# An adaLN block with gated convolution and differential attention: shorter lead of the high halves, a later head step, 1024-column pieces, tokens in two transfers, modulation in two bursts

## The chip, the cores and the metric

The kernel runs on one core of a Trainium2 chip. The metric is the device time of one execution in microseconds (us). Three runs of the kernel before gave 950.05, 951.05 and 951.22 us, a median of 951.05. Everything is float32 at the interface. The profile is of one further execution of the same program.

## The reference, cut to what matters

The input is 256 latent tokens `x` and 256 context tokens `ctx`, both of width 2048, with one condition vector each.

```python
shift, scale, gate = split(silu(c) @ w_ada + b_ada, 3)          # w_ada: 2048 x 6144
c_shift, c_scale, _ = split(silu(c_ctx) @ w_ada + b_ada, 3)
h  = rms(x)   * (1 + scale)   + shift
hc = rms(ctx) * (1 + c_scale) + c_shift
p   = h @ w_in                                                  # w_in: 2048 x 12288
pkv = hc @ w_in[:, K and V columns]                             # context gives keys and values only
q, k, v = heads(p);  k, v = concat with context's k, v;  q, k rotated by 2-D axial rope
a = softmax(q1 k1) - lam * softmax(q2 k2);  o = rms(a @ v) * subln_w * (1 - lam_init)
y_b = (o * silu(p[zb])) @ w_out_b                               # 8 heads, 2 x 64 wide
y_a = (gb * conv3(gc * xa) * silu(za)) @ w_out_a                # xa, gb, gc, za: 1024 columns each
m   = sigmoid(p[ga]) * y_a + sigmoid(p[gb]) * y_b
out = rms(x + gate * (m @ w_o)) * final_norm_w
```

## The kernel before, in words

Every large product is computed in three float32r passes. A weight piece is split into a high half (`hi`, a cast on ACT) and a low half (`lo`, piece minus `hi`, a subtraction on DVE). The activations are split in the same way, and TensorE (PE) sums hi times hi, hi times lo and lo times hi. `H` holds the split modulated latents, `hc` (tiles `hctx`) those of the context.

The weights stream from HBM in pieces of 512 KB, which SP issues. Pieces that are split go to tiles `raw` (`RAWB` = 5 buffers), pieces of `w_ada` for the modulation go to tiles `raw_ada` (`ADAB` = 6 buffers). Until the context tokens are transposed, the code allows one raw_ada and two raw buffers less, since context tokens lie in them.

The order of the program is a list `plan`, filled by `do(function)` and `use(piece, function)`, and walked by `run_plan`. Before each piece is used, `advance(done)` emits what is due ahead of it: the cast to `hi` of pieces up to `done + split - held`, the subtraction to `lo` of pieces up to one less, and DMA issues into every free buffer. Each engine executes its instructions in the order in which they are emitted, so this walk sets the order on ACT, DVE and SP as well as on PE. `split` is 1 at the start and `AHEAD` = 4 from the first key piece on; `held` counts the first pieces that are kept until the context needs them.

The stages in order of time are these. First the latent tokens (four transfers of 512 KB) are transposed (`transpose_tokens`), and their mean squares are taken on DVE. Four pieces of `w_ada` give scale and shift of row tile 0. The keys and values of row tile 0 come next (`first_keys`, `first_values`; pieces named `first`), in four pieces of one row tile by 512 columns; then the context tokens are transposed, and the same four pieces serve the context. After that the remaining 15 row tiles of 128 rows are taken in groups (`GROUPS`): row tiles 1, 2 and 3 one at a time, then six pairs. In each group `key_steps` and `value_steps` list the work, in halves j = 0 and 1 of 512 columns, and the modulation pieces of the next group (`ada_items`, tiles `ada`, `arow`, `adat`) are placed between these steps, two pieces at a time. At the end of a group's accumulation DVE adds each PSUM bank to `kT` or `vv`.

Then come the queries (`q`), and the stages zb, xa, gc, gb, za, each made of pieces of two row tiles by 512 columns, 24 matmuls per piece. The 16 units of attention (8 heads by 2 token halves) are woven into these pieces: a new unit starts every `ATTS` = 5 pieces, and its steps `scores`, `exps`, `shares`, `combine`, `probs_t`, `mix` follow at a lag of 0, 1, 2, 3, 4 and 6 pieces. `combine` (DVE) writes `e`, `probs_t` transposes it on PE (`aT`), and `mix` multiplies it with the values (`o`). The merge and the output projection end the kernel.

DMA completion is counted in eight semaphores (`DMAHW0` to `DMAHW7` in the order listings), taken in turn by the transfers of SP and ACT; a transfer waits until the earlier one with its semaphore has landed.

Of the kernel before, what the change touches and what calls it, by code (L numbers as in the profile page):

```python
# [10 lines left out]
F32 = mybir.dt.float32  # L11
F32R = mybir.dt.float32r
# [25 lines left out]
STAT = 2  # L38
NORM, LATE = 88, 96
GATE0, GATES = 97, 2.4  # L40
# [26 lines left out]
def block_kernel(ctx: ExitStack, tc: tile.TileContext, x, c, cx, c_ctx, w_ada, b_ada, w_in, conv_w,  # L67
# [42 lines left out]
    def piece(w, k0, nk, c0, name, dst=None):  # L110
        return (w, k0, nk, c0, 512, name, True, dst)

# [3 lines left out]
    room = {True: RAWB, False: ADAB}  # L116
    lead = {"split": 1, "held": 0}
    rest = []
# [4 lines left out]
    def run_plan():  # L123
# [6 lines left out]
        def advance(done):  # L130
            while True:
                n = state["hi"]
                if n in raws and n < done + lead["split"] - lead["held"] + 1:
                    nk, _, _, name, two, dst = loads[n][2:]
                    if two:
                        parts[n] = dst() if dst else (
                            wp.tile([P, nk, 512], F32R, tag="hi", name=f"hi_{name}", bufs=HIB), None)
                        A.copy(parts[n][0], raws[n])  # L138
                    state["hi"] += 1
                    continue  # L140
                n = state["lo"]
                two, dst = loads[n][6:] if n < state["hi"] else (False, None)
                if n < state["hi"] and n < done + (lead["split"] - lead["held"] if two or dst else AHEAD):
                    if two:
                        hi, lo = parts[n]
                        if not dst:
                            nk, name = loads[n][2], loads[n][5]
                            lo = wp.tile([P, nk, 512], F32R, tag="lo", name=f"lo_{name}")
# [38 lines left out]
    rot = one.tile([P, 2 * T], F32, tag="rot", name="rot")  # L187
    nc.scalar.dma_start(cst, consts[:, 0:C_COS])
    cosT, sinT = rot[:, 0:T], rot[:, T:2 * T]
# [5 lines left out]
    def load_tokens(s, t):  # L195
        for n in range(2):
            if s == 0:
                if n == 0:
                    whole = one.tile([P, 2, half], F32, tag=f"vv{t}", name=f"xin{s}{t}")
                xin = whole[:, n]  # L200
            else:
                pool, tag, bufs = ((wp, "raw", RAWB), (wp, "raw", RAWB), (p1, "ada", ADAB), (p1, "hctx", 2))[t * 2 + n]
                xin = pool.tile([P, half], F32, tag=tag, name=f"xin{s}{t}{n}", bufs=bufs)
            nc.sync.dma_start(xin, (x, cx)[s][0, t * P:(t + 1) * P, n * half:(n + 1) * half])
            xins[s, t, n] = xin

# [7 lines left out]
    cv = one.tile([NC, P], F32, tag="kT0", name="cv")  # L214
    vec = one.tile([NV, P], F32, tag="kT1", name="vec")
    nc.scalar.dma_start(cv[0:16, :], c.rearrange("b (k p) -> (b k) p", p=P))
    nc.scalar.dma_start(cv[16:32, :], c_ctx.rearrange("(k p) -> k p", p=P))
# [199 lines left out]
    def first_keys(parts, j, s):  # L417
        for ct in range(4):
            pb = bank(f"k_{j}{ct}{s}")
            key_mms(pb, parts, 0, ct, s, 0, True, True)  # L420
            A.copy(kT[j]()[:, ct, s, :], pb[:, s * T:(s + 1) * T])

    def first_values(parts, j, s):
        for b in (2 * s, 2 * s + 1):
            pb = bank(f"v_{j}{b}")
            value_mms(pb, parts, 0, b, 0, True, True)
            A.copy(vv[j]()[:, b, :], pb)

    def key_steps(k0, nk, j):

        box, held, last = {}, [], k0 + nk

        def step(kk, per, s, ct):
            parts = held[(kk - k0) // 2]
            if (s, kk) == (0, k0):
                box[ct] = bank(f"k{k0}_{j}{ct}")
            for i in range(per):
                key_mms(box[ct], parts, i, ct, s, kk + i, kk + i == k0, kk + i == last - 1)
            if s and kk + per == last:
                dst = kT[j]()[:, ct].rearrange("p s t -> p (s t)")  # L440
                V.tensor_tensor(dst, box[ct], dst, op=ALU.add)  # L441

        out = []
# [7 lines left out]
    def value_steps(k0, nk, j):  # L451
        box, held = {}, []

        def step(kk, per, b):
            if kk == k0:
                box[b] = bank(f"v{k0}_{j}{b}")
            for i in range(per):
                value_mms(box[b], held[-1], i, b, kk + i, kk + i == k0, kk + i == k0 + nk - 1)
            if kk + per == k0 + nk:
# [4 lines left out]
        for kk, per in cuts(k0, nk):  # L464
            out.append((piece(w_in[0], kk, per, V_OFF + j * 512, f"v{j}_{kk}"), held.append))
            out += [(None, lambda _, a=(kk, per, b): step(*a)) for b in range(4)]
# [69 lines left out]
    held = []  # L536
    for n, (off, j) in enumerate(((K_OFF, 0), (K_OFF, 1), (V_OFF, 0), (V_OFF, 1))):
        def first(parts, f=(first_keys, first_values)[n // 2], j=j):
            f(parts, j, 0)
            held.append((f, parts, j))  # L540
            lead["held"] += 1

        use(piece(w_in[0], 0, 1, off + j * 512, f"first{n}"), first)

# [3 lines left out]
    def first_context(n):  # L548
        f, parts, j = held[n]
        f(parts, j, 1)  # L550
        lead["held"] -= 1

# [13 lines left out]
    for n, g in enumerate(GROUPS[1:]):  # L566
        nxt, tails = [], {}
        if n + 2 < len(GROUPS):
            (scale, scale_end), (shift, shift_end) = ada_items(*GROUPS[n + 2], 1), ada_items(*GROUPS[n + 2], 0)
            nxt = scale + shift  # L570
        kv = key_steps(*g, 0) + key_steps(*g, 1) + value_steps(*g, 0) + value_steps(*g, 1)
        done, total = 0, len(nxt)
        for i, it in enumerate(kv):
# [393 lines left out]
```

## Time and profile before

| | us |
|---|---|
| median of three runs | 951.05 |
| lowest and highest run | 950.05 and 951.22 |
| profiled execution | 951.32 |
| its span, first to last instruction | 949.5 |
| PE busy in it | 922.2 |
| DVE busy in it | 647.9 |
| ACT busy in it | 422.0 |

The profiled execution's time is 1.8 us above its span; this is the launch around it. The page divides the span into 40 slices. Where an engine has idle time, the rows give it in brackets after the instruction that ended it, with the engine or transfer whose event released it. The granted clock of TensorE is given as a share of 2.4 GHz: 1.00 is that level, and 0.50 is 1.2 GHz.

### The profile page before, as it was taken

To read this page: it belongs to the slowest core of one execution; us is meant where nothing else is said; L and a number is where in the kernel's file an instruction comes from. 1 tells how busy PE (TensorE), PEld (TensorE's weight loads), DVE (VectorE), ACT (ScalarE), POOL (GpSimd) and SP (SyncE) were. 2 spreads that over 40 slices of the span, in tenths; PEclk is the share of its full clock that TensorE was granted. 3 is DMA by queue.
4 is the path that set the end of the run, shared out by engine and by line. 5 is a ranking of instruction groups with operands and counts; after the bars stand their busy time and mean duration, and the time that the engine had idled before them with its cause. 6 is when DMAs were issued, how large, how long until landed. Compare 5 with 4: busy or idle time off the path is not lost.

```text
span 949.5 us, 17652 instructions
## 1 busy us (share of the span) xinstructions
PE 922.2 (97%) x7308; PEld 853.1 (90%) x7308; DVE 647.9 (68%) x967; ACT 422.0 (44%) x623; POOL 1.9 (0%) x7
## 2 busy tenths in 40 slices
PE   8699999999999999999999999999999999999996
PEld 7577788888899999999999999999999999998885
DVE  3369866777758676686776866677767667756664
ACT  4442222123234466654765566543543344444442
POOL 0000000000000000000000000000000000000000
PEclk9799999999999999999999999999999999999999
DMA  9687966675366546545454645567987887867552
GB/s 287 207 245 250 342 223 218 214 241 156 89 190 182 179 137 197 156 135 169 149 172 133 180 154 164 167 227 252 312 270 240 304 296 242 288 213 266 178 177 89
DMA packets 123430, 196.76 MB, mean 207 GB/s; under 512 B 6125, under 2 KB 47446, under 8 KB 122838
## 3 DMA queue, kind: packets, MB, share of 16 engines
q1 hardware_dynamic: 122752, 194.40, 64.6%
q8 instruction: 57, 0.93, 0.4%
q10 hardware_dynamic: 598, 1.23, 0.3%
q14 instruction: 23, 0.19, 0.1%
HBM read 193.52 MB, written 2.10 MB: 206 GB/s over the span
## 4 chain that ended last, share of the span: by engine, by line
PE 89%; DVE 5%; DMA 3%; ACT 2%; SPq 1%; issue 1%; ACTq 0%; DVEq 0%
PE gb L484 13%; PE ga L484 10%; PE f L862 9%; PE v L408 9%; PE k L415 9%; PE za L484 5%; PE zb L484 5%; PE yb L484 5%; PE q L484 5%; PE ya L484 5%; PE gc L484 4%; PE xa L484 4%; PE ada L351 3%; DMA raw_first<-in_w_in_dram 1%; PE o L682 1%; SPq L167 1%
## 5 line engine op out<-in xcount | busy, mean ns | idle before, releaser
L484 PE MATMUL gb<-H,hi_gb 128*128 128x256 f32 x768 | 137.7, 281 | 0.0
L484 PEld LDWEIGHTS gb<-H,hi_gb 128*128 128x128 f32 x768 | 117.3, 188 | 0.8 <-issue 0.7
L484 PE MATMUL gb<-H,lo_gb 128*128 128x256 f32 x384 | 107.2, 279 | 0.0
L484 PE MATMUL ga<-H,hi_ga 128*128 128x256 f32 x512 | 90.9, 280 | 0.0
L484 PEld LDWEIGHTS ga<-H,hi_ga 128*128 128x128 f32 x512 | 78.1, 188 | 0.3 <-issue 0.2
L484 PEld LDWEIGHTS gb<-H,lo_gb 128*128 128x128 f32 x384 | 72.1, 188 | 0.0
L484 PE MATMUL ga<-H,lo_ga 128*128 128x256 f32 x256 | 71.4, 279 | 0.0
L138 ACT CAST hi_gb<-raw_gb 128x1024 fp32r<-128x1024 f32 x48 | 50.1, 1050 | 45.2 <-DMA raw_gb<-in_w_in_dram 24.8
L441 DVE TENSOR_TENSOR kT<-k,kT 128x512 f32<-128x512 f32 x72 | 47.7, 687 | 28.3 <-PE k L415 27.9
L149 DVE TENSOR_TENSOR lo_gb<-raw_gb,hi_gb 128x1024 fp32r<-128x1024 f32 x48 | 58.1, 1220 | 8.4 <-ACT hi_gb L138 4.6
L862 PE MATMUL f<-hi_o,M 128*128 128x512 f32 x192 | 60.6, 394 | 0.0
L461 DVE TENSOR_TENSOR vv<-v,vv 128x512 f32<-128x512 f32 x72 | 46.4, 686 | 15.7 <-PE v L408 15.6
L354 ACT COPY arow<-ada 128x256 f32<-128x256 f32 (+1 forms) x20 | 6.6, 330 | 112.0 <-PE ada L351 112.0
L484 PEld LDWEIGHTS ga<-H,lo_ga 128*128 128x128 f32 x256 | 48.1, 188 | 0.0
L484 PE MATMUL xa<-H,hi_xa 128*128 128x256 f32 x256 | 46.4, 283 | 0.0
L484 PE MATMUL za<-H,hi_za 128*128 128x256 f32 x256 | 46.4, 283 | 0.0
L415 PE MATMUL k<-H,hi_k 128*128 128x256 f32 x240 | 46.1, 289 | 0.1
L484 PE MATMUL gc<-H,hi_gc 128*128 128x256 f32 x256 | 46.2, 282 | 0.0
L812 DVE SCALAR_TENSOR_TENSOR gacc<-raw_gate,cT,gacc 128x512 f32<-128x512 f32 x60 | 45.0, 749 | 1.7 <-DMA raw_gate<-in_w_ada_dram 0.6
L484 PE MATMUL zb<-H,hi_zb 128*128 128x256 f32 x256 | 45.7, 281 | 0.0
L484 PE MATMUL yb<-OB,hi_yb 128*128 128x256 f32 x256 | 45.4, 279 | 0.0
L484 PE MATMUL q<-H,hi_q 128*128 128x256 f32 x256 | 45.3, 280 | 0.0
(243 smaller groups left out, 2410.1 us busy)
## 6 DMA issues: line engine op xcount, KB each, us to landing
raw_ada<-in_w_ada_dram SPq DMA_DIRECT2D x64, 512.0 KB, 6.3
raw_gb<-in_w_in_dram SPq DMA_DIRECT2D x48, 512.0 KB, 4.6
raw_ga<-in_w_in_dram SPq DMA_DIRECT2D x32, 512.0 KB, 5.0
raw_gate<-in_w_ada_dram SPq DMA_DIRECT2D x32, 512.0 KB, 5.3
raw_o<-in_w_o_dram SPq DMA_DIRECT2D x32, 512.0 KB, 5.0
raw_q<-in_w_in_dram SPq DMA_DIRECT2D x16, 512.0 KB, 3.7
raw_zb<-in_w_in_dram SPq DMA_DIRECT2D x16, 512.0 KB, 4.5
raw_xa<-in_w_in_dram SPq DMA_DIRECT2D x16, 512.0 KB, 3.7
```

Of the source, the lines that this page charges most:

```text
L138: A.copy(parts[n][0], raws[n])
L149: V.tensor_tensor(lo, raws.pop(n), hi.bitcast(F32), op=ALU.subtract)
L167: nc.sync.dma_start(raw, w[k0 * P:(k0 + nk) * P, c0:c0 + width].rearrange("(k p) n -> p k n", p=P))
L351: E.matmul(pa[q:q + 32, 0:width], cT[:, 2 * k:2 * k + 32], raw[:, i, :], start=k < 4, stop=k >= KT - 4)
L408: E.matmul(pb, l, r, start=first and n == 0, stop=last and n == 2)
L415: E.matmul(pb[:, s * T:(s + 1) * T], l[:, i, cs], r, start=first and n == 0, stop=last and n == 2)
L441: V.tensor_tensor(dst, box[ct], dst, op=ALU.add)
L461: V.tensor_tensor(dst, box[b], dst, op=ALU.add)
L484: E.matmul(out, l[:, i, cs], r, start=c + kk + i + n == 0, stop=c == 1 and kk + i == nk - 1 and n == 2)
L682: E.matmul(po[:, 0:P], aT[:, kb, :], vv[h // 4]()[:, kb, (h % 4) * P:(h % 4 + 1) * P], start=kb == 0, stop=kb == 3)
L812: V.scalar_tensor_tensor(acc, raw[:, i, :], cs, acc, op0=ALU.mult, op1=ALU.add)
L862: E.matmul(pb[:, 0:width], l, r[:, i, c0:c0 + width], start=k == 0 and n == 0, stop=k == KT - 1 and n == 2)
```

## The change

There are five edits.

- `lead["hi"]` is new: casts to `hi` run one piece ahead of the subtractions only from the queries on. Until then both have the same reach.
- `piece` gives 1024 columns when a piece has one row tile (`1024 // nk`). The tile keeps its form of 2 by 512 elements per partition; the second index is now the column half j instead of the row tile. This concerns `first` (two pieces instead of four) and the groups of row tiles 1, 2 and 3 (two pieces each instead of four). `key_steps` and `value_steps` of j = 1 then reuse the piece of j = 0.
- The latent tokens come in two transfers of 1 MB instead of four of 512 KB, and the constants `cst` are issued in the code after the memory for the vectors is taken; on ACT's queue `cst` stays first.
- The modulation pieces of a group of two row tiles are used four at a time (`range(len(scale))`) instead of two at a time.
- `probs_t` and `mix` move to lags 5 and 7; `NORM` and `LATE` move by one piece as well.

```diff
-NORM, LATE = 88, 96
+NORM, LATE = 89, 97
...
     def piece(w, k0, nk, c0, name, dst=None):
-        return (w, k0, nk, c0, 512, name, True, dst)
+        return (w, k0, nk, c0, 1024 // nk, name, True, dst)
...
-                if n in raws and n < done + lead["split"] - lead["held"] + 1:
+                if n in raws and n < done + lead["split"] - lead["held"] + lead["hi"]:
                     nk, _, _, name, two, dst = loads[n][2:]
                     if two:
                         parts[n] = dst() if dst else (
-                            wp.tile([P, nk, 512], F32R, tag="hi", name=f"hi_{name}", bufs=HIB), None)
+                            wp.tile([P, 2, 512], F32R, tag="hi", name=f"hi_{name}", bufs=HIB), None)
+                        if nk == 1:
+                            raws[n] = raws[n].rearrange("p k (a n) -> p (k a) n", a=2)
                         A.copy(parts[n][0], raws[n])
...
+        if s == 0:
+            whole = one.tile([P, 2, half], F32, tag=f"vv{t}", name=f"xin{s}{t}")
+            nc.sync.dma_start(whole.rearrange("p n d -> p (n d)"), x[0, t * P:(t + 1) * P, :])
...
             for i in range(per):
-                key_mms(box[ct], parts, i, ct, s, kk + i, kk + i == k0, kk + i == last - 1)
+                key_mms(box[ct], parts, i if nk > 1 else j, ct, s, kk + i, kk + i == k0, kk + i == last - 1)
...
-            out.append((piece(w_in[0], kk, per, K_OFF + j * 512, f"k{j}_{kk}"), held.append))
+            if nk > 1 or not j:
+                out.append((piece(w_in[0], kk, per, K_OFF + j * 512, f"k{j}_{kk}"), held.append))
...
-    for n, (off, j) in enumerate(((K_OFF, 0), (K_OFF, 1), (V_OFF, 0), (V_OFF, 1))):
-        def first(parts, f=(first_keys, first_values)[n // 2], j=j):
-            f(parts, j, 0)
-            held.append((f, parts, j))
+    for n, (off, f) in enumerate(((K_OFF, first_keys), (V_OFF, first_values))):
+        def first(parts, f=f):
+            for j in range(2):
+                f(parts, j, 0)
+            held.append((f, parts))
             lead["held"] += 1
...
-                for _ in range(2):
+                for _ in range(len(scale)):
                     use(*nxt[done])
                     done += 1
...
+    do(lead.update, {"hi": 1})
     do(load_late)
...
-        for lag, f in ((0, scores), (1, exps), (2, shares), (3, combine), (4, probs_t), (6, mix)):
+        for lag, f in ((0, scores), (1, exps), (2, shares), (3, combine), (5, probs_t), (7, mix)):
```

Three places show how the change moves instructions. The first is SP's queue at the start, with what each issue waits for (`first`: the pieces of row tile 0; `xin_24x`: context tokens). In the kernel before:

```order
8 L167 DMA raw_first_218<-in_w_in_dram 128x512 [waits DMAHW6_49]
9 L167 DMA raw_first_220<-in_w_in_dram 128x512 [waits DMAHW7_49]
10 L167 DMA raw_first_222<-in_w_in_dram 128x512 [waits DMAHW0_49]
11 L167 DMA raw_ada_1_0_224<-in_w_ada_dram 128x8x128 [waits DMAHW1_49]
12 L204 DMA xin_240<-in_ctx_dram 128x1024 [waits DMAHW2_49]
13 L204 DMA xin_242<-in_ctx_dram 128x1024 [waits DMAHW3_49]
14 L204 DMA xin_244<-in_ctx_dram 128x1024 [waits DMAHW4_49]
15 L204 DMA xin_246<-in_ctx_dram 128x1024 [waits DMAHW5_49]
16 L167 DMA raw_ada_1_8_248<-in_w_ada_dram 128x8x128 [waits DMAHW6_49,PE_49]
17 L167 DMA raw_ada_1_0_265<-in_w_ada_dram 128x8x128 [waits DMAHW7_49,PE_49]
18 L167 DMA raw_ada_1_8_292<-in_w_ada_dram 128x8x128 [waits DMAHW0_49,PE_49]
19 L167 DMA raw_first_331<-in_w_in_dram 128x512 [waits DMAHW1_49,DVE_49,Activation_49]
```

The same stretch of SP's queue in the changed kernel:

```order
7 L169 DMA raw_first_216<-in_w_in_dram 128x1024 [waits DMAHW4_49]
8 L169 DMA raw_first_218<-in_w_in_dram 128x1024 [waits DMAHW5_49]
9 L169 DMA raw_ada_1_0_220<-in_w_ada_dram 128x8x128 [waits DMAHW6_49]
10 L169 DMA raw_k_1_222<-in_w_in_dram 128x1024 [waits DMAHW7_49]
11 L205 DMA xin_238<-in_ctx_dram 128x1024 [waits DMAHW0_49]
12 L205 DMA xin_240<-in_ctx_dram 128x1024 [waits DMAHW1_49]
13 L205 DMA xin_242<-in_ctx_dram 128x1024 [waits DMAHW2_49]
14 L205 DMA xin_244<-in_ctx_dram 128x1024 [waits DMAHW3_49]
15 L169 DMA raw_ada_1_8_246<-in_w_ada_dram 128x8x128 [waits DMAHW4_49,PE_49]
16 L169 DMA raw_ada_1_0_263<-in_w_ada_dram 128x8x128 [waits DMAHW5_49,PE_49]
```

Before, the last quarter of `first` stood behind the context tokens and three modulation pieces, and waited for DVE and ACT besides. Now both halves of `first` stand ahead of them and wait for no engine; the key piece of row tile 1 has moved ahead of the context tokens too.

The second place is ACT between the modulation of row tile 0 and the first evacuations of keys (`arow`: modulation rows, `H`: modulated latents, `kT`: evacuated keys). Before:

```order
22 L327 COPY rstd<-rows_279 128x256 [waits PE_49]
23 L138 CAST hi_first_290<-raw_first_218 128x512 [waits DMAHW6_49]
24 L354 COPY arow_0_302<-ada_0_267 128x128 [waits PE_49]
25 L389 ACTIVATE H<-hf_288,shT 128x256 [waits DVE_49]
26 L138 CAST hi_first_321<-raw_first_220 128x512 [waits DMAHW7_49]
27 L138 CAST hi_first_323<-raw_first_222 128x512 [waits DMAHW0_49]
28 L138 CAST hi_first_333<-raw_first_331 128x512 [waits DMAHW1_49]
29 L421 COPY kT_349<-k_345 128x256 [waits DMAHW3_49,DMAHW2_49,PE_49]
```

The same place on ACT in the changed kernel:

```order
22 L329 COPY rstd<-rows_277 128x256 [waits PE_49]
23 L356 COPY arow_0_298<-ada_0_265 128x128 [waits PE_49]
24 L391 ACTIVATE H<-hf_286,shT 128x256 [waits DVE_49]
25 L141 CAST hi_first_317<-raw_first_216 128x1024 [waits DMAHW4_49]
26 L141 CAST hi_first_319<-raw_first_218 128x1024 [waits DMAHW5_49]
27 L423 COPY kT_335<-k_331 128x256 [waits DMAHW3_49,DMAHW2_49,PE_49]
```

The cast that stood ahead of `arow` now stands behind `H`, and the fourth cast, which stood ahead of the key evacuations, is gone; two casts of 1024 columns replace four of 512.

The third place is ACT in the middle of the head steps (`aT`: evacuation of the transposed probabilities, `e`: exponentials, `ojunk`: the square that follows `mix`). Before:

```order
207 L685 ACTIVATE ojunk_4022,ossq<-o_4016 128x128
208 L138 CAST hi_xa_12_4024<-raw_xa_12_3870 128x1024
209 L660 ACTIVATE e_4012<-e_4012,rr_4054 128x512
210 L138 CAST hi_xa_14_4058<-raw_xa_14_3901 128x1024
211 L138 CAST hi_gc_0_4089<-raw_gc_0_3944 128x1024
212 L675 COPY aT_4124<-aT_4119 128x512
213 L138 CAST hi_gc_2_4131<-raw_gc_2_3986 128x1024
214 L138 CAST hi_gc_4_4171<-raw_gc_4_4028 128x1024
215 L652 ACTIVATE e_4201,sums_4202<-sc_4162,mx_4161 128x512
```

The same unit in the changed kernel:

```order
199 L141 CAST hi_xa_12_3966<-raw_xa_12_3820 128x1024
200 L668 ACTIVATE e_3962<-e_3962,rr_3996 128x512
201 L693 ACTIVATE ojunk_4006,ossq<-o_4000 128x128
202 L141 CAST hi_xa_14_4008<-raw_xa_14_3851 128x1024
203 L141 CAST hi_gc_0_4039<-raw_gc_0_3887 128x1024
204 L141 CAST hi_gc_2_4074<-raw_gc_2_3936 128x1024
205 L683 COPY aT_4119<-aT_4114 128x512
206 L141 CAST hi_gc_4_4121<-raw_gc_4_3970 128x1024
207 L660 ACTIVATE e_4151,sums_4152<-sc_4105,mx_4104 128x512
```

One cast of a later piece, thus one piece of PE's work, has come between the scaling of `e` and the evacuation of `aT`. On PE the transposes `aT` now stand directly behind the `scores` matmuls of the next unit, with no piece between them.

## Rows read from the trace of the kernel before

**Rows 1.** Page, busy us, share of the span, instructions.
```profile
PE 922.2 (97%) x7308; PEld 853.1 (90%) x7308; DVE 647.9 (68%) x967; ACT 422.0 (44%) x623; POOL 1.9 (0%) x7
DMA packets 123430, 196.76 MB, mean 207 GB/s; under 512 B 6125, under 2 KB 47446, under 8 KB 122838
```
**Rows 2.** Waits of PE, whole span: us in total, times, longest us.
```profile
PE v L408 <- ACT kT L421: 8.7, 1, 8.7
PE aT L673 <- DVE e L665: 3.6, 3, 1.5
PE ada L351 <- DMA raw_ada<-in_w_ada_dram: 1.7, 2, 1.5
```
**Rows 3.** Chain that ended last: start us, us, what.
```profile
0.73 4.72 DMA cst<-in_consts_dram
...
28.83 5.58 DMA raw_first<-in_w_in_dram
```
**Rows 4.** Timeline of PE, start: start us, us, operation, idle before.
```profile
26.35 0.28 PE L415 MATMUL k<-H,lo_first 128*128 128x256 f32 x1
35.37 0.80 PE L408 MATMUL v<-hi_first,H 128*128 128x512 f32 x1 [8.75 <-ACT kT L421]
...
40.66 4.05 PE L312 MATMUL xt<-cst,xin 128*128 128x128 f32 x32
...
48.56 0.90 PE L415 MATMUL k<-hctx,hi_first 128*128 128x256 f32 x2 [0.82 <-ACT hctx L389]
...
52.55 0.50 PE L408 MATMUL v<-hi_first,hctx 128*128 128x512 f32 x1
...
55.47 0.27 PE L361 MATMUL adat<-cst,arow 128*128 128x128 f32 x1
...
60.71 1.08 PE L351 MATMUL ada<-raw_ada,cT 128*32 128x128 f32 x32
```
**Rows 5.** Timelines of ACT and DVE, context tokens.
```profile
39.12 1.22 DVE L304 SCALAR_TENSOR_TENSOR junk<-xin 128x1024 bf16<-128x1024 f32 x1
...
44.56 0.26 ACT L277 ACTIVATE r_w<-r_w 128x2 f32<-128x2 f32 x1
```
**Rows 6.** Stretches: busy us of each engine, PEclk, DMA share, GB/s.
```profile
8.00:28.00 20.00, 15.84 (x166) 13.18 (x164) 9.91 (x28) 8.38 (x18) 0.00 (x0) 1.00 1.09 337
28.00:36.00 8.00, 0.63 (x2) 0.53 (x3) 0.92 (x2) 1.57 (x5) 0.00 (x0) 0.70 1.00 285
57.00:103.00 46.00, 44.08 (x392) 35.43 (x395) 43.53 (x87) 12.91 (x28) 0.00 (x0) 1.00 0.84 263
103.00:241.00 138.00, 138.00 (x1056) 112.54 (x1049) 98.13 (x165) 33.31 (x52) 0.00 (x0) 1.00 0.70 220
```
**Rows 7.** SP's issue of the last two context tiles, and the last one's landing.
```profile
17.74 1.99 SPq L204 DMA_DIRECT2D xin<-in_ctx_dram  x2
...
DMA to landing us min/median/max: 9.5/9.5/9.5
```
**Rows 8.** Chain: keys with one burst ahead of them, and without any.
```profile
131.37 3.73 PE k L415 x30
...
241.33 11.31 PE k L415 x96
```
**Rows 9.** Modulation pieces: page's issues; SP and PE at the first pair.
```profile
raw_ada<-in_w_ada_dram SPq DMA_DIRECT2D x64, 512.0 KB, 6.3
...
88.61 0.37 SPq L167 DMA_DIRECT2D raw_v<-in_w_in_dram  x1
89.07 2.35 SPq L167 DMA_DIRECT2D raw_ada<-in_w_ada_dram  x4
...
95.30 0.64 PE L351 MATMUL ada<-raw_ada,cT 128*32 128x256 f32 x8 [1.52 <-DMA raw_ada<-in_w_ada_dram]
```
**Rows 10.** ACT, two casts; PE, its longest wait for `e`.
```profile
108.76 2.00 ACT L138 CAST hi_v<-raw_v 128x1024 fp32r<-128x1024 f32 x2
...
425.08 0.63 PE L673 MATMUL aT<-cst,e 128*128 128x128 f32 x4 [1.50 <-DVE e L665]
```

More of the change, by code (lines that the diff above doesn't have):

```diff
@@ L116, in block_kernel @@
     room = {True: RAWB, False: ADAB}
-    lead = {"split": 1, "held": 0}
+    lead = {"split": 1, "held": 0, "hi": 0}
     rest = []
@@ L146, in advance @@
                         if not dst:
-                            nk, name = loads[n][2], loads[n][5]
-                            lo = wp.tile([P, nk, 512], F32R, tag="lo", name=f"lo_{name}")
+                            lo = wp.tile([P, 2, 512], F32R, tag="lo", name=f"lo_{loads[n][5]}")
                         V.tensor_tensor(lo, raws.pop(n), hi.bitcast(F32), op=ALU.subtract)
@@ L187, in block_kernel @@
     rot = one.tile([P, 2 * T], F32, tag="rot", name="rot")
-    nc.scalar.dma_start(cst, consts[:, 0:C_COS])
     cosT, sinT = rot[:, 0:T], rot[:, T:2 * T]
@@ L195, in load_tokens @@
     def load_tokens(s, t):
[L196 to L201, printed above, removed]
+        if s == 0:
+            whole = one.tile([P, 2, half], F32, tag=f"vv{t}", name=f"xin{s}{t}")
+            nc.sync.dma_start(whole.rearrange("p n d -> p (n d)"), x[0, t * P:(t + 1) * P, :])
+            xins.update({(s, t, n): whole[:, n] for n in range(2)})
+        else:
+            for n in range(2):
                 pool, tag, bufs = ((wp, "raw", RAWB), (wp, "raw", RAWB), (p1, "ada", ADAB), (p1, "hctx", 2))[t * 2 + n]
                 xin = pool.tile([P, half], F32, tag=tag, name=f"xin{s}{t}{n}", bufs=bufs)
-            nc.sync.dma_start(xin, (x, cx)[s][0, t * P:(t + 1) * P, n * half:(n + 1) * half])
-            xins[s, t, n] = xin
+                nc.sync.dma_start(xin, cx[0, t * P:(t + 1) * P, n * half:(n + 1) * half])
+                xins[s, t, n] = xin
     for t in range(2):
@@ L215, in block_kernel @@
     vec = one.tile([NV, P], F32, tag="kT1", name="vec")
+    nc.scalar.dma_start(cst, consts[:, 0:C_COS])
     nc.scalar.dma_start(cv[0:16, :], c.rearrange("b (k p) -> (b k) p", p=P))
@@ L419, in first_keys @@
             pb = bank(f"k_{j}{ct}{s}")
-            key_mms(pb, parts, 0, ct, s, 0, True, True)
+            key_mms(pb, parts, j, ct, s, 0, True, True)
             A.copy(kT[j]()[:, ct, s, :], pb[:, s * T:(s + 1) * T])
@@ L425, in first_values, with key_steps @@
             pb = bank(f"v_{j}{b}")
-            value_mms(pb, parts, 0, b, 0, True, True)
+            value_mms(pb, parts, j, b, 0, True, True)
             A.copy(vv[j]()[:, b, :], pb)
-    def key_steps(k0, nk, j):
-        box, held, last = {}, [], k0 + nk
+    def key_steps(k0, nk, j, held):
+        box, last = {}, k0 + nk
         def step(kk, per, s, ct):
@@ L449, in key_steps, with value_steps @@
         return out
-    def value_steps(k0, nk, j):
-        box, held = {}, []
+    def value_steps(k0, nk, j, held):
+        box = {}
         def step(kk, per, b):
@@ L457, in step @@
             for i in range(per):
-                value_mms(box[b], held[-1], i, b, kk + i, kk + i == k0, kk + i == k0 + nk - 1)
+                value_mms(box[b], held[-1], i if nk > 1 else j, b, kk + i, kk + i == k0, kk + i == k0 + nk - 1)
             if kk + per == k0 + nk:
@@ L464, in value_steps @@
         for kk, per in cuts(k0, nk):
-            out.append((piece(w_in[0], kk, per, V_OFF + j * 512, f"v{j}_{kk}"), held.append))
+            if nk > 1 or not j:
+                out.append((piece(w_in[0], kk, per, V_OFF + j * 512, f"v{j}_{kk}"), held.append))
             out += [(None, lambda _, a=(kk, per, b): step(*a)) for b in range(4)]
@@ L536, in block_kernel @@
     held = []
-    for n, (off, j) in enumerate(((K_OFF, 0), (K_OFF, 1), (V_OFF, 0), (V_OFF, 1))):
-        def first(parts, f=(first_keys, first_values)[n // 2], j=j):
-            f(parts, j, 0)
-            held.append((f, parts, j))
+    for n, (off, f) in enumerate(((K_OFF, first_keys), (V_OFF, first_values))):
[3 more added lines that the diff above has]
+            held.append((f, parts))
             lead["held"] += 1
-        use(piece(w_in[0], 0, 1, off + j * 512, f"first{n}"), first)
+        use(piece(w_in[0], 0, 1, off, f"first{n}"), first)
     do(transpose_tokens, 1)
@@ L548, in first_context @@
     def first_context(n):
-        f, parts, j = held[n]
-        f(parts, j, 1)
-        lead["held"] -= 1
+        f, parts = held[n // 2]
+        f(parts, n % 2, 1)
+        lead["held"] -= n % 2
     (scale, scale_end), (shift, shift_end) = ada_items(*GROUPS[1], 1), ada_items(*GROUPS[1], 0)
@@ L570, in block_kernel @@
             nxt = scale + shift
-        kv = key_steps(*g, 0) + key_steps(*g, 1) + value_steps(*g, 0) + value_steps(*g, 1)
+        keys, values = ([[], []] if g[1] > 1 else [[]] * 2 for _ in range(2))
+        kv = [it for j in range(2) for it in key_steps(*g, j, keys[j])]
+        kv += [it for j in range(2) for it in value_steps(*g, j, values[j])]
         done, total = 0, len(nxt)
```

## The prediction

> **What bounds the kernel now.** I read the page first. PE is busy 97% of the span and DVE 68% [rows 1]. PE is thus the bound, and a change that leaves its matmuls as they are can win only what PE loses: the 27 us between its 922.2 busy and the span of 949.5, matmuls at half clock, and switches between kinds of matmul. The list of PE's waits came second. One wait of 8.7 us in the first values is the largest, three waits of the transposes for `e` make 3.6 us, and modulation pieces that land late 1.7 us [rows 2]. The reader is to see that the first is one event, not a habit.
>
> The chain and PE's timeline show what made it. PE ends the first keys at 26.6 us and begins the first values at 35.37 [rows 4]. The fourth piece of `first` is issued only at 28.83 and lands 5.6 us later [rows 3]; its cast stands ahead of the key evacuations on ACT, and the values wait for these to free a bank. The stretches then show a second price: in 28 to 36 us the mean clock is 0.70 [rows 6], so it fell during the idle time. The twelve value matmuls take 5.3 us (35.37 to 40.66), where the same twelve for the context take 2.9 (52.55 to 55.47) [rows 4].
>
> After 57 us there are two regimes. In 57 to 103 us, the single row tiles, DVE is busy 43.5 of 46 us and PE 44.1: both are near their limit. In 103 to 241 us, the pairs, PE is busy all of the time [rows 6].
>
> **The start: two pieces of 1024 columns for four of 512, and casts later.** All of `first` now fits the raw buffers and is issued ahead of the context tokens. Ahead of its end stand the same bytes as of the third piece before, and 256 KB more, which are 0.8 us at the 337 GB/s of 8 to 28 us [rows 6]. I leave the end of the first keys at 26.6 us. The values then start 8.75 us earlier and run at full clock, which saves 2.4 us more: they end at 29.5 instead of 40.66, 11.2 us earlier.
>
> What is late next is the context. From the start of its transposes to `r_w` on ACT it is 3.9 us, and from there to the first context keys 4.0 [rows 4, 5]. With the same distances `r_w` comes at 33.4 and the context keys at 37.4 instead of 48.56: **11.2 us**. The cover for this is the token stream. The last context tile is issued at about 19.3 us and lands 9.5 later [rows 7], at 28.8. Now 0.8 MB more stands ahead of it (the key piece of row tile 1 and the last quarter of `first`), 2.3 us, so 31.1. DVE's last mean square of 1.2 us [rows 5] ends at 32.3, before 33.4. The cover is 1.1 us; beyond it every us costs one.
>
> Behind that, the stream has no pause any more. Up to the last modulation piece of row tile 2, SP issues 27 times 512 KB, 14.2 MB. In 8 to 28 us 6.7 MB move [rows 6]; with 1.7 MB before that, my estimate from the same rate and a start at 3 us, 5.8 MB are left at 28 us. At 285 to 337 GB/s [rows 6] they have moved by 45 to 48 us. PE uses these pieces 12.2 us after the context keys begin (48.56 to 60.71 [rows 4]), thus at 49.6. I take no wait; bounds 0 and +3.
>
> The first keys may themselves move. The cast that waited for a transfer ahead of `arow` is gone; I give that at most 1 us. Against it, the latent tokens now stand in transfers of 1 MB with rows of 8 KB, and PE's first transposes need `cst`, which landed 4.72 us after its issue at 0.73 [rows 3]. At worst it lands behind both token transfers: 2.1 MB at 337 GB/s from 1.7 us on, at 8.0, 2.5 us later. Only 592 of 123430 packets have 8 KB or more [rows 1], so the trace hardly shows the case. I take 0 for the first keys; bounds -1 and +2.5. The Trainium skill, "DMA: Bandwidth & Descriptors", section "Queues, rings and completion order", says that each DMA engine goes round the queues packet by packet. By it packets of twice the size would hold back ACT's small transfers for longer, up to twice, and the sum would be about 1.5 us worse, an estimate from that page's rule.
>
> **Two bursts instead of four.** Thirty key matmuls together with the switches of a burst take 3.73 us; 96 without one take 11.31, thus 3.53 for thirty [rows 8]. A burst costs 0.20 us beside its own matmuls. Six groups lose two bursts each; in the five of them where PE is the bound this is 5 x 2 x 0.2 = **2.0 us**. A burst now empties four of six buffers. The third and fourth shift piece are issued during the scale burst, 0.5 to 1 us into it, and land 6.3 us after their issue [rows 9]. They are wanted some 9.8 us into it (2 us of burst, nine steps of six matmuls or 0.7, and two pieces of 0.5), so this is hidden by 2.5 us or more; bounds -2.4 and +3.
>
> For the first pair the modulation stands under a single row tile, whose steps are half as long. Before, an issue of `raw_v` at 88.61 stood ahead of four modulation pieces, which went out only from 89.07 on, and PE waited 1.52 us [rows 9]. Now nothing but modulation stands between the third and fourth shift piece. They land at 6.8 and 7.3 us by the same 6.3, and are wanted at about 6.6 and 7.1; and DVE is nearly full there [rows 6], so that PE's gain may become a wait for DVE. I take **0.5 us**; bounds 0 and -1.5.
>
> **1024 columns in the single row tiles.** Twelve subtractions become six of double length; DVE's additions and PE's matmuls stay. I take 0; bounds -0.6 and +1, about one cast to either side [rows 10].
>
> **Casts no longer one piece ahead.** A subtraction may now wait for its own cast of 1.0 us [rows 10]. ACT is busy 12.9 of 46 us among the single row tiles [rows 6], and most casts stand behind a modulation copy that PE releases early, while DVE stands behind its additions. I take 0; the other end is the third rival.
>
> **Head steps.** The transposes get one more piece of PE's work, 24 matmuls or 2.8 us, between `combine` and themselves; the longest of the three waits was 1.5 us [rows 2, 10]. All **3.6 us** go; bounds -3.6 and, if DVE's backlog is met elsewhere, 0. `scores` and the transposes now touch, so one return to the split matmuls falls away in 15 units. At one side of a burst's switches, 0.1 us, this would be 1.5; since transposes and scores are not the same kind of matmul I take half, **0.7 us**, bounds 0 and -1.5.
>
> **Sum.** 11.2 + 2.0 + 0.5 + 3.6 + 0.7 = 18.0 us, from 951.3 of the profiled execution to 933.3. The median of the runs lies 0.3 below the profiled execution, so I predict 933.0 us.
>
> **Rivals.** First, the start gives part back: context tokens or modulation pieces land late at 30 to 50 us, or the clock falls again as in 28 to 36 us [rows 6] while PE waits in pieces between 29.5 and 37.4. For it speaks a stream without a pause and a cover of 1.1 us. Against it, the fall followed one idle time of 8.75 us, and no gap here should be longer than 2 us, my estimate. Price: the 3 us of context keys and 2.9 of values at half clock, or as much waiting, 5 to 6 us: 938.5.
>
> Second, DVE takes the place of the waits in the heads, since it is 68% busy over all: the 4.3 us of that part stay, 937.3. Against it, PE shows no wait for a subtraction there.
>
> Third, on the other side: without the lead, ACT's cast and DVE's subtraction stand in series in the whole stage of keys and values. There are 30 pieces, 6 single and 24 of pairs; exposed in each, the cast costs 30 us, and the time is 963. It decides from 60% of the casts on, 18 of 30, where gain and loss meet. In 103 to 241 us DVE is 71% busy and ACT 24% [rows 6], which leaves room for that wait; this speaks against it.
>
> Fourth, `cst` is held back by the tokens, and all of the start moves by 1.5 to 2.5 us: 935.
>
> **Chances.** The forecast, 928 to 936.5, has 0.64; the first rival 0.17, the second 0.08, the third 0.04, the fourth 0.07. The range takes in the first, second and fourth at their prices and most of the gains beyond the sum: 927 to 941. A measurement of this kernel tells 0.2%, 2 us, from no change: faster 0.94, same 0.02, slower 0.04.
>
> **What would show it.** The wait of the values for `kT` is gone; the first values start near 26.6 us and the context keys near 37.4; the clock stays at 1.00 in 28 to 44 us. A pair takes 0.4 us less, and the waits for `e` are gone. Wrong would be a new wait for context tokens or `ada` of more than 2 us or a lower clock before 50 us (first rival), PE waiting for subtractions among the heads (second), PE waiting for `lo` among keys and values (third), or PE's first transposes after 9 us (fourth).

## The result

The changed kernel takes 929.6 us, the median of four runs from 929.23 to 930.12; four runs of the kernel before gave a median of 950.57. The ratio is 0.978, with a 95% interval of 0.976 to 0.980. The profiled execution has a span of 927.6 us, against 949.5 before.

The page of the changed kernel, busy us and share of the span, then the clock row and the packets, answers to [rows 1]:

```profile
PE 914.7 (99%) x7308; PEld 852.0 (92%) x7308; DVE 646.3 (70%) x959; ACT 418.2 (45%) x615; POOL 1.9 (0%) x7
...
PEclk9999999999999999999999999999999999999998
...
DMA packets 121989, 196.75 MB, mean 212 GB/s; under 512 B 5965, under 2 KB 47286, under 8 KB 121142
```

PE does the same 7308 matmuls, and its idle time in the span has gone from 27 us to 13. Its waits, in total, times and longest, which answer to [rows 2]:

```profile
PE warm L236 <- POOL cT L233: 1.0, 1, 1.0
PE k L417 <- ACT hctx L391: 0.8, 1, 0.8
PE k L417 <- DVE lo_first L151: 0.8, 1, 0.8
PE k L417 <- ACT hi_first L141: 0.6, 1, 0.6
PE ada L353 <- DMA raw_ada<-in_w_ada_dram: 0.5, 1, 0.5
PE v L410 <- DVE kT L443: 0.3, 1, 0.3
PE cols L246 <- DMA cv<-in_c_ctx_dram: 0.2, 1, 0.2
```

The waits of 8.7 and 3.6 us are gone, and nothing over 1.0 us has taken their place. PE's timeline answers to [rows 4]; it gives start, length, operation and, in brackets, the idle time before it:

```profile
20.83 0.51 PE L417 MATMUL k<-H,hi_first 128*128 128x256 f32 x2 [0.59 <-ACT hi_first L141]
...
24.79 0.40 PE L410 MATMUL v<-hi_first,H 128*128 128x512 f32 x1
...
27.60 3.66 PE L314 MATMUL xt<-cst,xin 128*128 128x128 f32 x32
...
35.10 0.91 PE L417 MATMUL k<-hctx,hi_first 128*128 128x256 f32 x2 [0.82 <-ACT hctx L391]
...
43.28 0.91 PE L417 MATMUL k<-H,hi_k 128*128 128x256 f32 x2
```

The context keys begin at 35.10 instead of 48.56, 13.5 us earlier, where I had predicted 11.2. The stretches of the changed kernel, with the columns of [rows 6]:

```profile
28.00:36.00 8.00, 7.05 (x93) 6.14 (x92) 4.34 (x17) 5.53 (x13) 0.00 (x0) 1.00 1.05 292
36.00:44.00 8.00, 7.86 (x86) 6.29 (x85) 3.05 (x7) 7.49 (x17) 0.00 (x0) 1.00 1.06 338
43.00:90.00 47.00, 46.53 (x437) 37.49 (x430) 44.24 (x84) 13.35 (x25) 0.00 (x0) 1.00 0.96 295
```

The clock stays at 1.00 where it was 0.70, and the single row tiles (43 to 90 us) now keep the weight stream at a share of 0.96. The chain gives the pairs' distance and the head steps, which answer to [rows 8] and [rows 10]:

```profile
103.48 11.20 PE v L410 x48
114.68 1.86 PE ada L353 x32
...
130.40 11.20 PE v L410 x48
...
157.39 11.20 PE v L410 x48
...
342.72 0.59 PE aT L681 x4
...
359.24 0.59 PE aT L681 x4
```

Read along the stages, before against after, the gain is 13.5 us at the first keys of row tile 1 (56.74 to 43.28), 15.7 at the values of the first pair (119.17 to 103.48), 18.8 at the queries (263.7 to 244.9), and 22.0 at the output projection (850.9 to 828.9). It is made in four places and not given back.

### The profile page after: what moved, and what is told of

Read it like the earlier page. It is cut to its first block, busy times and chain, and to the rows that moved or that the text cites. A ratio compares the mean times of both kernels' runs of the same rounds, so it can differ in the third digit from the quotient of the medians.

```text
span 927.6 us, 17602 instructions
## 1 busy us (share of the span) xinstructions
PE 914.7 (99%) x7308; PEld 852.0 (92%) x7308; DVE 646.3 (70%) x959; ACT 418.2 (45%) x615; POOL 1.9 (0%) x7
## 4 chain that ended last, share of the span: by engine, by line
PE 92%; DVE 5%; DMA 1%; ACT 1%; issue 0%; ACTq 0%; SPq 0%; DVEq 0%
PE gb L488 15%; PE ga L488 10%; PE f L870 10%; PE v L410 8%; PE k L417 7%; PE zb L488 5%; PE gc L488 5%; PE za L488 5%; PE xa L488 5%; PE yb L488 5%; PE q L488 5%; PE ya L488 5%; PE ada L353 2%; PE o L690 2%; DVE kT L443 2%; DVE vv L464 1%
## 5 line engine op out<-in xcount | busy, mean ns | idle before, releaser
L443 DVE TENSOR_TENSOR kT<-k,kT 128x512 f32<-128x512 f32 x72 | 45.2, 683 | 3.5 <-PE k L417 3.4
L488 PE MATMUL ya<-U,hi_ya 128*128 128x256 f32 x256 | 45.6, 281 | 0.0
```

The source lines that it names most:

```text
L488: E.matmul(out, l[:, i, cs], r, start=c + kk + i + n == 0, stop=c == 1 and kk + i == nk - 1 and n == 2)
```

## The experiments

Each run has its own median; the changed kernel's is 929.6 us. The kernel before ran beside them with medians of 950.25 to 950.68.

**The 1024-column pieces alone.** The kernel before with this one edit and the lines that belong to it in `advance`, `key_steps`, `value_steps` and the code of `first`:

```diff
-        return (w, k0, nk, c0, 512, name, True, dst)
+        return (w, k0, nk, c0, 1024 // nk, name, True, dst)
```

> The kernel before with the pieces of 1024 columns alone; tokens in four transfers, casts one piece ahead, bursts of two, lags 4 and 6. Theory A: the whole wait of 8.75 us, the half clock behind it and the advance of the context go with this edit: 11 to 12 us less than before, 938.5 to 939.5, context keys at about 37. Theory B: without the later casts and the tokens in two transfers the context tokens land too late, and only part of it comes: over 942.

Measured: 939.51 us, ratio 0.989 (0.987 to 0.990), thus 11.1 us by this edit alone. PE's waits of this run:

```profile
PE aT L681 <- DVE e L673: 3.6, 3, 1.5
PE adat L363 <- ACT arow L356: 2.6, 2, 1.9
```

The wait for `kT` is gone, the wait for `e` is still there, and the modulation copy `arow` still stands behind a cast that waits for its transfer. So the wide pieces remove the stall of the first values, and nothing else of the change is needed for that. The wait of 1.52 us at the modulation of the first pair [rows 9] is gone with them too: of the waits for `ada` 0.2 us are left, all of it at the start. (A piece of one row tile had 256 KB before and has 512 KB now; the 512 KB in the description of the kernel before hold for the other pieces.)

**All but the 1024-column pieces.** The other four edits with pieces of 512 columns. With these the casts' shorter reach would be zero pieces at the start, so in this kernel it is held to at least one:

```diff
-                if n in raws and n < done + lead["split"] - lead["held"] + lead["hi"]:
+                if n in raws and n < done + max(lead["split"] - lead["held"] + lead["hi"], 1):
```

> The changed kernel with pieces of 512 columns for single row tiles again (four pieces of first); the other four edits stay, but the cast of the piece in use is always allowed. Theory A: the fourth piece of first does not fit the three buffers; it is issued at about 23 us behind the context tokens, lands at about 33, its cast stands ahead of the key evacuations, the values wait some 9 us and run at half clock: 940 to 942. Theory B (the later casts alone had cured it): the first values start by 26 us and the time is below 932.

Measured: 946.67 us, ratio 0.996 (0.995 to 0.997). The stall of the first values is back, as expected; but the time is some 5 us above my estimate. The waits of this run show a second stall:

```profile
PE v L408 <- ACT kT L421: 9.3, 1, 9.3
PE ada L351 <- DMA raw_ada<-in_w_ada_dram: 5.1, 2, 4.7
```

SP's queue shows what it is. SP waits for DVE, which adds values from 80.88 to 85.74; the value piece is issued at 86.36, and only behind it four modulation pieces go out:

```profile
86.36 0.37 SPq L167 DMA_DIRECT2D raw_v<-in_w_in_dram  x1
86.84 2.25 SPq L167 DMA_DIRECT2D raw_ada<-in_w_ada_dram  x4
```

PE's timeline of the same run has the burst that wanted them:

```profile
87.60 1.50 PE L351 MATMUL ada<-raw_ada,cT 128*32 128x256 f32 x24
93.78 0.98 PE L351 MATMUL ada<-raw_ada,cT 128*32 128x256 f32 x8 [4.68 <-DMA raw_ada<-in_w_ada_dram]
```

The burst's last piece was issued at 86.84, 0.8 us before the burst began, and landed 6.9 us later. The eight matmuls behind the idle time take 0.98 us instead of the 0.64 they take elsewhere; the granted clock had fallen as well, it is 0.50 in 94 to 97 us. It is the wait of 1.52 us of [rows 9], three times as long.

**The same, with bursts of two.** Is this second stall made by the bursts of four?

```diff
-                for _ in range(len(scale)):
+                for _ in range(2):
```

> The changed kernel with pieces of 512 columns (as in the run with 512 columns, 946.7 us, with the reach of the cast held to at least one piece as there), and besides the modulation pieces used two at a time again. It tells what the 4.7 us wait for ada at the first pair came from. Theory A, the burst of four meets a queue in which a value piece stands ahead of the modulation pieces and waits for DVE: with bursts of two the third and fourth piece are wanted half a group later, the wait falls back to 1.5 us as in the kernel before, and the time is 946.7 + 3.5 for the bursts - 3.2 = 947.0. Theory B, the wait comes from the later start alone and has nothing to do with the bursts: it stays at 4 to 5 us, 950. The wait of 9.3 us for kT at the first values stays under both.

Measured: 945.13 us, ratio 0.994 (0.992 to 0.995). Its waits:

```profile
PE v L408 <- ACT kT L421: 8.8, 1, 8.8
PE ada L351 <- DMA raw_ada<-in_w_ada_dram: 1.8, 1, 1.8
```

Theory A holds: the wait falls from 4.7 to 1.8 us. The time is 1.9 us below its 947.0; 1.1 us of that are there before the bursts come in, at the first keys of row tile 1 (53.49 us against 54.61). On narrow pieces bursts of four thus lose 1.5 us (946.67 against 945.13), where on wide ones they gain 3.5 (next run). The two edits belong together: with wide pieces half as many weight pieces of the single row tiles are issued between the modulation pieces. Under row tile 3 of the changed kernel SP issues seven modulation pieces in a row, and PE's burst waits for none:

```profile
65.79 11.42 SPq L169 DMA_DIRECT2D raw_ada<-in_w_ada_dram  x7
...
76.14 1.93 PE L353 MATMUL ada<-raw_ada,cT 128*32 128x256 f32 x32
```

**Bursts of two in the changed kernel.** The same edit, in the changed kernel:

> The changed kernel with the modulation pieces used two at a time again. Theory A (the forecast's term): a burst costs 0.20 us beside its matmuls, so 5 pairs lose 2 x 0.2 each: 929.6 + 2.0 = 931.6, and the distance between the values of two pairs grows from 26.98 to 27.4 us. Theory B (the distances of the two traces, 27.74 before and 26.98 after): a burst costs about 0.38 us beside its matmuls, the distance goes back to 27.7 and the time to 933.4 to 934.3.

Measured: 933.07 us, ratio 0.982 (0.981 to 0.983): 3.5 us worse. Its chain:

```profile
103.91 11.20 PE v L410 x48
115.11 1.00 PE ada L353 x16
...
131.65 11.20 PE v L410 x48
```

The distance of two pairs is 27.74 us again, as before the change, where the changed kernel has 26.99. Two bursts less are worth 0.75 us, 0.37 each, and not the 0.20 of the prediction.

**Bursts of one piece.** To find the price of a burst from a third point, the same line with `range(1)`:

> The changed kernel with the modulation pieces used one at a time: eight bursts for a pair instead of two. Theory A (0.20 us a burst): six more bursts in each of 5 pairs, 6.0 us, 935.6, distance 28.2. Theory B (0.38 us a burst): 11.4 us, 941, distance 29.3. A third theory, that the gain came from the time at which modulation pieces are fetched and not from the number of bursts: then one at a time spreads the transfers most evenly and the time is not above that with two at a time.

Measured: 942.49 us, ratio 0.992 (0.990 to 0.993). Its chain:

```profile
119.49 0.57 PE ada L353 x8
...
148.59 0.57 PE ada L353 x8
```

The pair takes 29.10 us; four bursts more than with bursts of two cost 1.36, 0.34 each. The lengths say where this is: 8, 16 and 32 matmuls take 0.57, 1.00 and 1.86 us, that is 0.43 per piece and 0.14 besides. So a burst costs 0.14 us inside its own row and 0.20 in the rows around it.

**The head steps as before.** The changed kernel with the old lags:

```diff
-NORM, LATE = 89, 97
+NORM, LATE = 88, 96
...
-        ... (3, combine), (5, probs_t), (7, mix)):
+        ... (3, combine), (4, probs_t), (6, mix)):
```

> The changed kernel with probs_t and mix at lags 4 and 6 again. Theory A (the forecast's terms): the three waits for e, 3.6 us, come back and the 0.7 us of touching scores and transposes are lost: 933.9. Theory B (five pieces take 16.46 us before and 16.52 after where nothing waits): the waits come back, but 16 units get 0.05 us cheaper each: 932.4 to 932.9. Theory C: DVE is the bound there and only passes the wait on: 930 or less.

Measured: 932.95 us, ratio 0.982 (0.981 to 0.984): 3.35 us worse. The wait is back, to the tenth of [rows 2]:

```profile
PE aT L681 <- DVE e L673: 3.6, 3, 1.5
```

**One more piece of lag.** With lags of 6 and 8 the wait is still gone, but `scores` and `aT` no longer touch:

```diff
-NORM, LATE = 89, 97
+NORM, LATE = 90, 98
...
-        ... (3, combine), (5, probs_t), (7, mix)):
+        ... (3, combine), (6, probs_t), (8, mix)):
```

> The changed kernel with probs_t and mix at lags 6 and 8, so that the transposes no longer touch the scores but stay late enough for e. Theory A: 15 units lose 0.05 us each of what touching saved: 930.3. Theory B: touching costs 0.05 us a unit, so the time falls by 0.8 us to 928.8, five pieces take 16.46 us, and there is no wait for e.

Measured: 930.09 us, ratio 0.979 (0.978 to 0.981), not to be told from the changed kernel. Its chain shows why:

```profile
346.26 0.44 PE aT L681 x4
...
359.36 0.43 PE sc L648 x2
359.79 2.93 PE xa L488 x24
362.72 0.44 PE aT L681 x4
```

Five pieces take 16.46 us here (346.26 to 362.72) and 16.52 in the changed kernel (342.72 to 359.24, above). Where the transposes touch the scores they take 0.59 us instead of 0.44: the switch is paid there. From the first query to the first matmul of the output projection both kernels take 583.9 us (245.49 to 829.42 here, 244.93 to 828.87 in the changed kernel). Both expectations gave touching a price of some sign; over the whole stage it has none that can be seen.

**The latent tokens in four transfers.**

```diff
-            nc.sync.dma_start(whole.rearrange("p n d -> p (n d)"), x[0, t * P:(t + 1) * P, :])
+            for n in range(2):
+                nc.sync.dma_start(whole[:, n], x[0, t * P:(t + 1) * P, n * half:(n + 1) * half])
```

> The changed kernel with the latent tokens in four transfers of 512 KB again. Theory A (the forecast, 0 for this edit): 929.6, the first keys start at 20.8 us as in the changed kernel. Theory B: the transfers of 1 MB brought the modulation pieces forward by about 1 us, since the third transfer had to wait for the constants; the first keys start at 21.8 and the time is 930.6. Theory C (the constants suffered from the large packets): the first keys start 0.5 us earlier, 929.1.

Measured: 930.64 us, ratio 0.980 (0.978 to 0.981). The medians are 1.0 us apart and the intervals overlap, so the time alone does not decide. In the trace the first keys start at 22.0 us, 1.2 later. The changed kernel's own trace is the earliest of six whose kernels share its start (the others are those with bursts of two and of one, with both other lags, and with the additional pair): their first keys start at 20.83 to 21.56, always 13.07 us after PE's first transposes. So two transfers are worth 0.5 to 1.2 us there. The chain of this run names the transfer:

```profile
1.65 5.18 DMA cv<-in_c_ctx_dram
...
7.62 9.17 DMA raw_ada<-in_w_ada_dram
...
16.93 0.64 PE ada L354 x16
```

It is the third modulation piece. It goes out at 7.62, hardly later than in the changed kernel (7.4), but lands 9.17 us later, there 7.1. With four token transfers the third one waits 3.9 us on SP until the constants have landed, and tokens are issued until 6.3 us, just ahead of the modulation pieces; with two they are issued by 1.6. This is what theory B said. PE uses the third piece at 16.93 and the fourth at 18.77 here, at 15.81 and 17.58 in the changed kernel.

**Casts ahead from the start.**

```diff
-    lead = {"split": 1, "held": 0, "hi": 0}
+    lead = {"split": 1, "held": 0, "hi": 1}
```

> The changed kernel with the casts one piece ahead from the start, as before the change. Theory A: the lead only matters at the start, where the cast of the first piece stands ahead of a modulation copy again: H comes 1.4 to 2.3 us later, the keys 0.4 to 1.3 us: 930.0 to 930.9, and nothing changes among the pairs. Theory B: the lead helped among the single row tiles, where DVE waits for casts: then the time falls below 929.

Measured: 931.11 us, ratio 0.980 (0.978 to 0.981): 1.5 us above the changed kernel. The intervals of the ratios overlap, but none of the four runs (930.91 to 931.35) lies among those of the changed kernel. The first keys start at 21.62 instead of 20.83, and that is not the casts' doing. The matmuls `warm`, the same in both kernels, happened to take longer ahead of PE's transposes; here and in the changed kernel:

```profile
0.99 7.54 PE L236 MATMUL warm<-cT 128*128 128x128 f32 x40 [0.99 <-POOL cT L233]
...
0.99 6.42 PE L236 MATMUL warm<-cT 128*128 128x128 f32 x40 [0.99 <-POOL cT L233]
```

From the first transposes (8.63 and 7.76) to the first keys it is 13.0 us here and 13.1 there. What the casts cost comes behind that:

```profile
PE adat L363 <- ACT arow L356: 1.3, 2, 0.7
...
45.53 1.04 ACT L141 CAST hi_k<-raw_k 128x1024 fp32r<-128x1024 f32 x1
46.48 0.25 ACT L356 COPY arow<-ada 128x128 f32<-128x128 f32 x1
```

The modulation copy stands behind a cast that was emitted ahead, and waits until the cast, and the cast's transfer, are done. The first of the two waits, 0.5 us at 20.19, makes the first values 0.2 us later, counted from the first transposes. The second, 0.7 us at 46.79, stands in row tile 1, where the copy runs at 44.47 in the changed kernel, ahead of that cast. Counted in the same way, the values of the first pair are 0.75 us late and the queries 1.0. So this trace shows 0.8 to 1.0 of the 1.5 us between the medians; where the rest is stays open.

**Row tiles 2 and 3 as a pair.** DVE is 44.2 of 47 us busy in 43 to 90 us of the changed kernel. Does it bound that stretch?

```diff
-GROUPS = [(k, 1) for k in range(4)] + [(k, 2) for k in range(4, 16, 2)]
+GROUPS = [(k, 1) for k in range(2)] + [(k, 2) for k in range(2, 16, 2)]
```

> The changed kernel with row tiles 2 and 3 taken as a pair instead of one at a time; 929.6 us is the changed kernel's median. DVE is 44 of 47 us busy in 43 to 90 us there, but PE waits only 0.8 us in it (0.5 for a modulation piece, 0.3 for an addition). Theory A, PE bounds this stretch now: what a pair saves is two modulation bursts (four of 32 matmuls become two), 0.3 to 0.4 us each, less 0.8 us at most of waits that go too: 928.0 to 929.3, and DVE falls by 16 additions of 0.68 us, 11 us. Theory B, the weight stream bounds it as soon as more is asked of it: the pair wants four more modulation pieces (2 MB, 7 us at 294 GB/s) under row tile 1, where the stream is already at a share of 1.02. Then PE waits for ada 3 to 7 us near 57 us and the time is 932 to 936.

Measured: 931.63 us (five runs, 929.34 to 932.60), ratio 0.979 (0.978 to 0.981): not faster, and by the interval not surely slower. The stretches of this run:

```profile
43.00:57.00 14.00, 10.47 (x111) 7.46 (x102) 8.29 (x18) 4.38 (x9) 0.00 (x0) 1.00 1.08 343
...
43.00:90.00 47.00, 43.47 (x354) 34.48 (x348) 35.20 (x64) 12.31 (x21) 0.00 (x0) 1.00 0.87 284
```

DVE loses 9 us of work and PE does not become faster: it waits 3.5 us for `ada` at four places between 44 and 54 us, while the stream runs at a share of 1.08. Theory B is right on what is late next; it comes earlier than the 57 us expected, and the time is just below its range: 931.6 against 932. Because a new wait came with the relief, this run alone does not say whether DVE bounded the stretch. The changed kernel's own row does: PE is busy 46.53 of the 47 us there at full clock, and waits 0.34 us for DVE, so relief of DVE could have won no more than 0.5 us.

## Why the prediction was right

The time came out 3.4 us below the 933.0 predicted, inside the forecast's own range. The mechanisms were those named; sizes were off. Between the two profiled executions the gain is 21.9 us (951.32 to 929.42), 3.9 more than the sum of 18.0: the start gave 2.3 more, the bursts 1.5 and the first pair 1.0, and the head steps gave 1.0 less.

**The start, 11.2 us predicted, 13.5 in the trace.** The step that was mis-sized is "I leave the end of the first keys at 26.6 us". The first values start at 24.79, 1.8 us earlier than that. The runs give two causes, which had got 1 us at most, and nothing: the copy `arow` no longer stands behind a cast, and the tokens come in two transfers. They act on the same thing, since the cast holds `arow` above all while it waits for its own transfer, and that comes earlier with two transfers (the cast starts at 20.74 with four, at 18.93 with two). With the wide pieces alone the first values start at 27.68; later casts bring them to 25.98 (the run with four token transfers), two transfers to 25.87 (the run with casts ahead, although its `warm` matmuls took 1.1 us longer than the changed kernel's), both to 24.79. Beside the two transfers, then, the casts are worth only 0.2 us at the first values. A part of the 1.8 is luck of this execution: in the six traces with this start the first keys lie 0.7 us apart, and this one is the earliest. Another 0.4 is the way from the context's transposes to `r_w`, 3.5 us instead of 3.9. The parts behind that held: values of 2.8 us at full clock, and 4.0 from `r_w` to the context keys.

**The stream.** I took no wait behind the context keys, and there is none. The clock stays at 1.00 and DVE waits 0.36 us for the last context tile. The first rival did not come. The run with the additional pair shows how near it was: four more modulation pieces in that stretch cost 3.5 us of waiting.

**The bursts, 2.0 us predicted, 3.5 measured.** The failed step is "A burst costs 0.20 us beside its own matmuls". Comparing the keys around a burst with keys without one finds only what lies outside its row. Another 0.14 lies inside, as part of the burst's 1.00 us, and it too is paid once per burst. The lengths of bursts of one, two and four pieces separate the two; the trace before had only bursts of two in the pairs. The 2.5 us of cover were right in kind but smaller: the modulation pieces land 7.1 us after their issue in the changed kernel, not 6.3 [rows 9], and the parts named for the 9.8 us at which the third shift piece is wanted add up to 9.3 (9.4 in the trace). One wait of 0.5 us is left, under the first pair, where a value piece goes out just ahead of the last shift piece:

```profile
91.75 0.37 SPq L169 DMA_DIRECT2D raw_v<-in_w_in_dram  x1
...
97.55 0.64 PE L353 MATMUL ada<-raw_ada,cT 128*32 128x256 f32 x8 [0.49 <-DMA raw_ada<-in_w_ada_dram]
```

**The first pair, 0.5 us.** Its wait went from 1.52 us to nothing, so 1.0 more than predicted; no new wait took its place there. That it depends on the wide pieces, the prediction implied with "nothing but modulation stands between"; the seven modulation pieces in a row show it, and the runs with 512 columns show the price where it is not so, 4.7 us and a lower clock.

**Head steps, 3.6 + 0.7 us predicted, 3.3 in the trace, 3.35 by the run with the old lags.** The waits of 3.6 us went, as said. The 0.7 for touching was a guess between two bounds, and the lower one, 0, is what the runs show. Rival two, DVE's backlog met elsewhere, did not come.

**1024 columns in the single row tiles and casts without the lead, 0 each.** The casts' term was 0.8 to 1.5 us too low, by the trace and by the medians: I had looked only for what the lead protects, and among the row tiles not for what stands behind a cast. PE waits for no `lo` among the keys and values after the first, so the third rival had nothing for it.

**`cst` held back by the tokens.** The fourth rival came, but small. `cst` lands 5.5 to 5.8 us after its issue in the nine traces with two token transfers and 4.7 to 5.0 in the three with four, the small transfer `cv` 5.7 to 6.1 and 5.1 to 5.4. In the changed kernel:

```profile
1.66 5.82 DMA cv<-in_c_ctx_dram
```

PE's first transposes start at 7.8 to 8.6 us in the nine and at 7.2 to 7.5 in the three, short of the 9 us named as the sign. A part of this are the `warm` matmuls, 6.3 to 7.5 us long in the nine and 6.1 to 6.4 in the three; no run shows why. The 0.5 to 1.2 us that two transfers are worth are what is left after it. The Trainium skill, "DMA: Bandwidth & Descriptors", section "Queues, rings and completion order", has the engines go round the queues packet by packet; the 0.6 us on `cv` agree with it in direction, but not with the 1.5 us that I had estimated from it. They do not show that the size of the packets is the cause: with four transfers the last two wait for `cst`, so only half of the tokens' bytes are issued before it has landed.

**The sum.** Taken one by one, by the medians, the edits are worth 11.1 (wide pieces, added to the kernel before) and 1.0, 1.5, 3.5 and 3.35 (tokens, casts, bursts and lags, taken from the changed kernel), 20.4 of the 21.0 us. They do not all add up in any order: the four without the wide pieces bring 3.9 us, not 9.4, most of it because of the second stall: with it, bursts of four lose 1.5 us where they gain 3.5 in the changed kernel.

No run beats the changed kernel. What the remaining 13 us of PE's idle time are made of was not pursued beyond the waits shown.

## What to carry to other kernels

An engine that is nearly full bounds a stretch only if another one waits for it: read the waits first, and the busy share after them. The price of a switch between kinds of work has a part inside the row of the work itself, which shows only when the same work appears in bursts of different length. On an in-order queue ask of every instruction that may wait what stands behind it: here PE lost 0.5 to 1.9 us at a time to a cast ahead of a copy on ACT, and 0.5 to 4.7 us to a value piece ahead of modulation pieces on SP. Before you put a difference between two traces down to an edit, see how far the same stretch moves between kernels that share it: the start moved by 0.7 us here, as much as the earlier casts had seemed to cost.

## What the runs showed of the hardware

- The narrow modulation matmuls (32 columns of stationary data) cost 0.34 to 0.37 us per burst among the float32r ones, for bursts of 8, 16 and 32: 0.57, 1.00 and 1.86 us for the burst itself, of which 0.14 do not grow with it, and 0.20 in the rows around it.
- Transposes directly behind the scores take 0.59 us for four, and 0.44 behind split matmuls; the stage as a whole takes 583.9 us either way.
- The more modulation pieces are issued in a row, the longer one takes to land: a median of 5.6 us with bursts of one, 6.2 to 6.7 with two (four traces) and 6.9 to 7.3 with four (seven traces).
- After an idle time of 4.68 us in the run with 512 columns eight matmuls take 0.98 us, and 0.64 elsewhere; the granted clock is 0.50 in the 94 to 97 us behind it.
- The 40 matmuls `warm` at the start, the same in every kernel, take 6.1 to 7.5 us in the twelve traces.
